# A decayed running sum behind a matrix product: the last four column blocks turned on TensorE, and the entry cut into finer pieces

## The chip, the cores and the metric

The kernel runs on one core of one Trainium2 chip. A core has five engines that work side by side, each through its own list in order: TensorE (PE, matmuls; its weight loads are shown as PEld), VectorE (DVE), ScalarE (ACT), GpSimd (POOL) and SyncE (SP, which here only issues transfers). 16 DMA engines move data between the main memory and the on-chip memory SBUF; TensorE writes into PSUM, a second on-chip memory of eight banks of 512 fp32 columns per partition. The metric is the device time of one execution in microseconds (us).

## The reference

```python
B, S, D = (16, 2048, 1024)
xw = x @ w                                   # x: (B, S, D), w: (D, D), float32
out[:, 0, :] = xw[:, 0, :]
for t in range(1, S):
    out[:, t, :] = decay * out[:, t - 1, :] + xw[:, t, :]    # decay: one factor per column
```

A matrix product, then along the time axis of each batch entry a recurrence with one decay factor per output column.

## The kernel before

**Tiling.** The 16 x 2048 rows are 64 chunks of 512 time steps. A chunk's product has 1024 columns, cut into eight slots n = 0 to 7 of 128 columns. A slot's column blocks are taken so that four times 32 columns of the output, 128 apart, make its 128 partitions. Slots 0 to 3 fill the lower half of the columns and slots 4 to 7 the upper half. The work of one slot is a step. In all groups but the last, a step covers two chunks (T = 1024 columns of PSUM, two banks); the last two chunks are worked one by one (T = 512), so that there are 31 x 8 + 16 = 264 steps. Negative numbers count steps from the end: -8 to -1 are the last chunk's slots.

**Into TensorE.** `load` fetches x on GpSimd's queue, cast to bf16. `turn` transposes it on VectorE in 32x32 blocks, reading pairs of bf16 as one fp32, and `part` copies it into `xt`, even and odd rows apart (ScalarE in the long run, both engines in the entry). `load_w` fetches the weights in pieces into the space of the output tiles, and `settle` copies them into `wsb`, as bf16, one copy for each row group k and half of the columns. A step is eight matmuls (k = 0 to 7) for each chunk.

**The recurrence.** PSUM holds the product with columns on partitions and time along the free axis. Slots of one kind (here called plain) are scanned by VectorE straight out of PSUM, 1024 steps in one `tensor_tensor_scan` (line 194). The others are paired: ScalarE copies the product to `xs` and multiplies the even steps by the decay, GpSimd adds these to the odd ones (line 174), VectorE scans the odd steps alone with the squared decay (line 180, half as long), and ScalarE and GpSimd fill in the even ones (lines 158 and 208). A plain slot's PSUM banks come free with VectorE's scan, a paired slot's with ScalarE's reads. `flips` names the steps that are the other kind than usual. The squared decays are in `dec2`, a PSUM tile that takes a bank.

**Out.** `back` transposes the result in 32x32 blocks on VectorE into an output tile, of which there are four in turn; when a half's four slots are there, `store` issues four transfers on SyncE, one for each group of 32 partitions, in runs of 128 columns (512 bytes). The last chunk's upper half is stored by two slots at a time, in runs of 64 columns (256 bytes).

**PSUM.** Of the eight banks, `ps` has three buffers of two banks in turn, `spare` one bank and `dec2` one.

**Order.** Every instruction is issued through `pin`, which keeps the order in which the program names it. That order is a list written by hand, `agenda`, of deeds for each step: letter and number, where P, S, C and B are a step's pairing, scan, completion and transposition back, T, X and Y the turning and copying of a chunk, W and w the weights' copies on VectorE and ScalarE, E, F and G the entry's turns and copies by halves of a chunk, M and U the first loads, D the decays and L one more load of x. Entry -99 is what comes before the first step, and steps without an entry follow `usual`. An engine takes its share of the list in this order and waits where an operand or a buffer isn't there. In the entry, TensorE first runs 34 matmuls on zeros (line 262), then chunk 0 for slots 0 to 3 (slot 3 in `spare`), by halves for the even k, then chunk 1 for slots 0 to 2, and slot 3's second half in the first of the `ps` buffers to come free.

Of the kernel before, what the change touches and what calls it, by code (L numbers as in the profile page):

```python
# [9 lines left out]
FP32 = mybir.dt.float32  # L10
# [15 lines left out]
def kernel(  # L26
# [60 lines left out]
        assert chunks[g[0]][0] == chunks[g[1]][0]  # L87

    dec = const.tile([128, K], FP32, name="dec")
    dec2 = psp.tile([128, 512], FP32, name="dec2")  # L90
    wsb = const.tile([128, K, K, NQ, P], BF16, name="wsb")
    wcols = wsb.rearrange("p k (h r) q i -> p k h q r i", h=2)

# [13 lines left out]
            in_=_ap(x, [[D, P], [P * D, j1 - j0], [1, CQ]],  # L107
                    (b * S + t0 + j0 * P) * D + q * CQ)))

    def turn(c, j0=0, j1=NJ):  # L110
        if c not in xw_of:
            xw_of[c] = ring(sb, "xw", 2, [128, M, NJ, P, 2], BF16)
        src = xb_of[c][:, j0:j1].rearrange("p j c -> p (j c)").bitcast(FP32)
        dst = xw_of[c].rearrange("p m j i e -> p (m j i e)").bitcast(FP32)
        pin(nc.vector.transpose(  # L115
            out=dst.rearrange("p (m j i) -> p j m i", m=M, i=P)[:, j0:j1],
            in_=src.rearrange("p (j m c) -> p j m c", m=M, c=P)))

    def part(c, copy, m0, m1, j0=0, j1=NJ):
        if c not in xt_of:  # L120
# [15 lines left out]
    class Tile:  # L136

        def __init__(self, g, n, ps, ot, there):  # L140
            self.b, self.t0 = chunks[g[0]]
            self.T = TL * len(g)
            self.n, self.ps, self.ot, self.there = n, ps, ot, there
            self.final = g == [nch - 1]
            self.paired = n % R != R - 1
            if len(tiles) in flips or len(tiles) - len(slots) in flips:
                self.paired = not self.paired
            self.so = ring(sb, "so", 4, [128, 2 * TL + 2])
            self.prev = None if self.t0 == 0 else last[n]
            if self.t0 + self.T < S:  # L150
                last[n] = const.tile([128, 1], FP32, name=f"keep{n}", bufs=2)
                self.keep = last[n]
            else:
                self.keep = None
# [22 lines left out]
        def scan(self):  # L177
            T, n, so = self.T, self.n, self.so
            if self.paired:
                pin(nc.vector.tensor_tensor_scan(  # L180
                    out=so[:, 3:T + 2:2],
                    data0=dec2[:, n:n + 1].to_broadcast([128, T // 2]),
                    data1=self.xs[:, 1:T:2],
                    initial=0.0 if self.prev is None else self.prev,
                    op0=ALU.mult,
                    op1=ALU.add,
                ))
            else:
                parts = self.ps if isinstance(self.ps, tuple) else (self.ps,)
                size = T // len(parts)  # L190
                before = 0.0 if self.prev is None else self.prev
                for i, ps in enumerate(parts):
                    t = 2 + i * size
                    pin(nc.vector.tensor_tensor_scan(  # L194
                        out=so[:, t:t + size],
                        data0=dec[:, n:n + 1].to_broadcast([128, size]),
                        data1=ps,
                        initial=before,
                        op0=ALU.mult,
                        op1=ALU.add,  # L200
                    ))
                    before = so[:, t + size - 1:t + size]
# [7 lines left out]
            if self.keep is not None:  # L210
                pin(nc.scalar.copy(out=self.keep, in_=so[:, T + 1:T + 2]))  # L211

        def back(self):
            T, n = self.T, self.n
            pin(nc.vector.transpose(  # L215
                out=self.ot[:, :, n % R * P:(n % R + 1) * P],
                in_=self.so[:, 2:T + 2].rearrange("p (i t) -> p i t", t=P)))
            self.there.add(n)
            size = 2 if self.final and n >= R else R
            n0 = n // size * size  # L220
            if self.there.issuperset(range(n0, n0 + size)):
                self.store(n0, n0 + size)

        def store(self, n0, n1):
            c0 = n0 % R * P
            size = (n1 - n0) * P
            for q in (0, 2, 1, 3):
                pin(nc.sync.dma_start(
                    out=_ap(out, [[D, P], [P * D, self.T // P], [1, size]],
                            (self.b * S + self.t0) * D + n0 // R * CH + q * CR + c0),  # L230
                    in_=self.ot[quad(q), :, c0:c0 + size]))


# [24 lines left out]
    rows = const.tile([128, 2, P], FP32, name="rows")  # L258
    pin(nc.vector.memset(idle, 0.0))  # L259
    pin(nc.vector.memset(rows, 0.0))  # L260
    for _ in range(34):
        pin(nc.tensor.matmul(out=spare, lhsT=idle[:, 0:128], rhs=idle, start=True, stop=True))  # L262
    H = NJ // 2
    halves = ((0, H), (H, NJ))
# [11 lines left out]
    def load_part(i):  # L276
        load_w(nc.gpsimd, *((0, 0, M // 2, M), (0, 1), (1, 0), (1, 1))[i])

    def settle_one(i, copy):
        settle(i // 8, i // 4 % 2, i % 4, copy)  # L280

    def decays(i):
        pin(nc.vector.transpose(out=cols, in_=rows))
        pin(nc.vector.tensor_copy(
            out=dec.rearrange("p (h r) -> p h r", h=2), in_=cols[:, :, 0:R]))
        pin(nc.vector.tensor_tensor(out=dec2[:, 0:K], in0=dec, in1=dec, op=ALU.mult))


    slots = [(g, n) for g in groups[:-1] for n in range(K)]
# [3 lines left out]
    def turn_and_load(c):  # L293
# [16 lines left out]
        "w": lambda i: settle_one(i, nc.scalar.copy),  # L310
        "M": load_half,
        "U": load_part,
        "E": lambda i: turn(i // 2, *halves[i % 2]),
        "F": lambda i: part(i // 2, nc.vector.tensor_copy, 0, 2, *halves[i % 2]),
        "G": lambda i: part(i // 2, nc.scalar.copy, 2, M, *halves[i % 2]),
        "f": lambda i: part(i // 2, nc.vector.tensor_copy, 2, M, *halves[i % 2]),
        "D": decays,
        "L": lambda i: load(*loads.pop(0)) if loads else None,
    }
    agenda = {  # L320
        -99: "M0 M1 U0 U1 M2 M3 U2 U3 L L L W0 w1 E0 F0 G0 w3 W2 E1 F1 G1 W4 w5 W6 w7 E2 F2 D G2 E3 F3 G3 W8 W9 W10 W11",
        0: "w12 L L w13 P0 S0",
        1: "w14 L P1 L",
        2: "S1 W15 P2 B0 S2",
        3: "T2 L S3 C0 C1 C2",
        4: "L P4 X2 L Y2 L B2 T3 B1 L",
        5: "P5 C3 X3 L S4",
        6: "B3 L Y3 S5 L P6 C5 C4 T4",
        7: "S7 S6 X4 L C7 C6 B5 B4 B7",
        8: "",  # L330
        9: "P8 B6 S8 P9 L L T5 C8",
        10: "P10 L L S9 L C9 L B8",
        11: "X5 S10 L C10 S11 B9",
        12: "P12 L B11 B10 C11 Y4",
        13: "P13 S12 T6 Y5 C12 L",
        14: "S13 P14 C13 L B12 L L",
        15: "S15 X6 S14 C14 B13",
        16: "L P16 B14 B15 Y6 L L",
        -16: "P-16 B-17 S-16 C-16 C-17",
        -15: "P-15",  # L340
        -14: "S-15 B-18 B-16 P-14",
        -13: "P-13 S-14 S-13 B-15",
# [6 lines left out]
        -6: "P-6 B-10 S-7 C-7 B-8",  # L349
        -5: "P-5 S-6 S-5",  # L350
        -4: "C-6 B-7 B-5 P-4 B-6",
        -3: "P-3 S-4 S-3",
        -2: "P-2 S-2 C-4 C-3 B-4",
        -1: "B-3 P-1 S-1 B-2 C-5 B-1 C-1 C-2",
    }
    flips = (0, 1, -2, -15, -8)
    later = {10: ["Y4"]}
    for c in range(5, nch):
        first = c // 2 * K
# [20 lines left out]
            deeds[deed[0]](int(deed[1:] or 0))  # L380

    perform(agenda[-99].split())
    for step, (g, n) in enumerate(slots):
        T = TL * len(g)
        if n % R == 0:
            ot, there = ot_tile(NJ * len(g)), set()
        if step == 0:
            heads = [ring(psp, "ps", 3, [128, T]) for _ in range(3)]
            firsts = [ps[:, 0:TL] for ps in heads] + [spare]
            for j0, j1 in halves:  # L390
                for k in range(0, K, 2):
                    for i in range(R):
                        matmul(firsts[i], i, k, xt_of[0], j0 * P, j1 * P)
            for k in range(1, K, 2):
                for i in range(R):
                    matmul(firsts[i], i, k, xt_of[0])
            for j0, j1 in halves:
                for i in range(3):
                    for k in range(K):
                        matmul(heads[i][:, TL:T], i, k, xt_of[1], j0 * P, j1 * P, j0 * P)  # L400
        if step < R:
            if n < 3:
                ps, second = heads[n], heads[n][:, TL:T]
            else:
                second = ring(psp, "ps", 3, [128, TL])
                ps = (spare, second)
            if n >= 3:
                for k in range(K):
                    matmul(second, n, k, xt_of[1])
        else:  # L410
            if len(g) == 2 or n % R < 3:
                ps = ring(psp, "ps", 3, [128, T])
            else:
                ps = ring(psp, "spare", 1, [128, TL])
            for k in range(K):
                for l, c in enumerate(g):
                    matmul(ps[:, l * TL:(l + 1) * TL], n, k, xt_of[c])
        tiles.append(Tile(g, n, ps, ot, there))
        left = step - len(slots)
        do = agenda.get(step, agenda.get(left) if left >= -2 * K else None)  # L420
        perform(usual(step) if do is None else do.split())
    assert not loads
# [28 lines left out]
```

## Time and profile before

| | us |
|---|---|
| time, median of 3 runs (lowest to highest) | 915.06 (914.53 to 915.75) |
| the profiled execution's own time | 914.25 |
| its span, from the first to the last instruction | 912.5 |
| TensorE, VectorE busy | 891.3, 826.0 |
| ScalarE, GpSimd busy | 685.8, 664.4 |
| start of the dummy matmuls; of the first real one | 1.20; 11.20 |
| end of the last matmul; of the last work on VectorE | 901.6; 905.6 |
| moved by DMA, mean rate | 204.49 MB, 224 GB/s |

A row of the timeline names the start, the time that the instructions of the row take together, engine, line, operation, what it writes and reads, the shape and the count; in brackets stands how long the engine was idle before and what ended that. The end of a matmul is modelled: one of 512 columns starts every 0.216 us while its row says about 0.38. A row of the table by stretches names the stretch, its length, busy us and count of instructions for PE, PEld, DVE, ACT and POOL, the clock granted to TensorE as a share of full speed, the mean busy share of the DMA engines (above 1 where packets of two queues are counted at once) and what they moved in GB/s. The slices cut the span into 40 equal parts; a digit is a share in tenths.

### The profile page before, as it was taken

What the parts mean: (1) busy time and instruction counts of PE and PEld (TensorE: products, weight loads), DVE (VectorE), ACT (ScalarE), POOL (GpSimd) and SP (SyncE); (2) the same over time, 40 slices, a digit from 0 to 9 for tenths busy, and PEclk for the clock granted to TensorE, in tenths of its full rate; (3) what the DMA queues carried; (4) which work ended last, traced back from release to release, by engine and by line L of the source; (5) the groups of instructions that cost most, each with busy time, mean ns of one, the idle gap of its engine ahead of it and who ended that gap; (6) DMA issues with size and microseconds to landing.
All of it is one profiled execution on the core that took longest, in us unless ns stands there. A gap on an engine that the chain in (4) does not pass through costs nothing.

```text
span 912.5 us, 11926 instructions
## 1 busy us (share of the span) xinstructions
PE 891.3 (98%) x4088; PEld 408.5 (45%) x4170; DVE 826.0 (91%) x613; ACT 685.8 (75%) x950; POOL 664.4 (73%) x764
## 2 busy tenths in 40 slices
PE   8899999999999999999999999999999999999995
PEld 4444444444444444444444444444444444444442
DVE  4999999999999999999999999999999999999986
ACT  3778887877877777778778778778778778777753
POOL 8688878777777777777677777777787776776552
PEclk9999999999999999999999999999999999999998
DMA  9999999999999999999999999999999999999668
GB/s 170 166 220 215 215 230 235 256 250 255 247 237 255 247 237 224 230 233 231 223 235 227 224 231 229 230 226 231 227 224 230 231 230 224 232 229 207 151 151 219
DMA packets 406253, 204.49 MB, mean 224 GB/s; under 512 B 12976, under 2 KB 405936, under 8 KB 406192
## 3 DMA queue, kind: packets, MB, share of 16 engines
q1 hardware_dynamic: 268848, 134.76, 59.5%
q0 software_dynamic: 137344, 68.96, 56.8%
q8 instruction: 32, 0.52, 0.2%
q14 instruction: 29, 0.24, 0.1%
HBM read 138.42 MB, written 134.22 MB: 299 GB/s over the span
## 4 chain that ended last, share of the span: by engine, by line
PE 90%; DMA 3%; POOL 2%; issue 2%; DVE 2%; ACT 1%; SPq 0%; DVEq 0%; POOLq 0%
PE ps L126 90%; DMA xb<-in_x_dram 2%; POOL xb L105 1%; DMA ot<-in_w_dram 1%; DVE so L194 1%; DVE xw L115 1%; POOL ot L245 1%; PE spare L126 0%; DMA out_dram<-ot 0%; DVE so L180 0%; POOL so L208 0%; ACT xt L123 0%; DVE ot L215 0%; POOL xs L174 0%; ACT xs L168 0%
## 5 line engine op out<-in xcount | busy, mean ns | idle before, releaser
L126 PE MATMUL ps<-xt,wsb 128*128 128x512 bf16 (+1 forms) x4011 | 874.2, 377 | 9.0 <-DVE so L194 2.6
L126 PEld LDWEIGHTS <-wsb 128*128 128x128 bf16 x4136 | 404.6, 98 | 485.7 <-issue 5.6
L174 POOL TENSOR_TENSOR xs<-h,xs 128x512 f32<-128x512 f32 (+1 forms) x193 | 245.3, 1271 | 195.5 <-ACT h L158 88.3
L168 ACT COPY xs<-ps 128x1024 f32<-128x1024 f32 (+1 forms) x193 | 191.6, 993 | 158.8 <-PE ps L126 149.3
L215 DVE STREAM_TRANSPOSE ot<-so 128x1024 f32<-128x1024 f32 (+1 forms) x264 | 302.7, 1184 | 1.9 <-POOL so L208 1.1
L208 POOL TENSOR_TENSOR so<-h,xs 128x512 f32<-128x512 f32 (+1 forms) x193 | 244.3, 1266 | 34.5 <-ACT h L158 18.1
L123 ACT COPY xt<-xw 128x2048 bf16<-128x2048 bf16 (+1 forms) x128 | 239.8, 1875 | 7.5 <-DVE xw L115 7.5
L105 POOL DMA_DIRECT2D xb<-in_x_dram x264 | 174.1, 660 | 2.0 <-POOLq L435 0.9
L158 ACT ACTIVATE h<-so,dec 128x512 f32<-128x512 f32 (+1 forms) x193 | 147.1, 763 | 36.0 <-DVE so L180 32.1
L115 DVE STREAM_TRANSPOSE xw<-xb 128x2048 f32<-128x2048 f32 (+1 forms) x66 | 146.7, 2222 | 6.1 <-DMA xb<-in_x_dram 6.1
L180 DVE TENSOR_TENSOR_SCAN so<-dec,keep,xs 128x512 f32<-128x512 f32 (+1 forms) x99 | 121.6, 1229 | 29.8 <-POOL xs L174 29.6
L180 DVE TENSOR_TENSOR_SCAN so<-dec,xs 128x512 f32<-128x512 f32 x94 | 114.8, 1222 | 31.3 <-POOL xs L174 28.2
L158 ACT ACTIVATE h<-ps,dec 128x512 f32<-128x512 f32 (+1 forms) x193 | 131.8, 683 | 0.0
L194 DVE TENSOR_TENSOR_SCAN so<-dec,ps 128x1024 f32<-128x1024 f32 x33 | 74.5, 2261 | 0.0
L194 DVE TENSOR_TENSOR_SCAN so<-dec,keep,ps 128x1024 f32<-128x1024 f32 (+1 forms) x33 | 73.4, 2225 | 0.0
L211 ACT COPY keep<-so 128x1 f32<-128x1 f32 x136 | 25.1, 187 | 0.3 <-DVE so L194 0.3
L173 ACT COPY so<-keep 128x1 f32<-128x1 f32 x99 | 19.0, 192 | 0.7 <-DVE ot L215 0.7
L171 POOL MEMSET so<- 128x1 f32 x94 | 11.0, 117 | 3.2 <-DVE ot L215 3.2
L262 PE MATMUL spare<-idle 128*128 128x512 bf16 x34 | 10.2, 473 | 1.2 <-DVE idle L259 1.2
L126 PE MATMUL spare<-xt,wsb 128*128 128x512 bf16 (+1 forms) x43 | 11.2, 359 | 0.1
L245 POOL DMA_DIRECT2D ot<-in_w_dram x16 | 9.0, 561 | 2.4 <-issue 0.7
L253 ACT COPY wsb<-ot 128x512 bf16<-128x512 bf16 x6 | 3.4, 615 | 5.7 <-DMA ot<-in_w_dram 5.7
(18 smaller groups left out, 20.3 us busy)
## 6 DMA issues: line engine op xcount, KB each, us to landing
out_dram<-ot SPq DMA_DIRECT2D x248, 512.0 KB, 10.6
xb<-in_x_dram POOLq DMA_DIRECT2D x248, 256.0 KB, 7.8
out_dram<-ot SPq DMA_DIRECT2D x12, 256.0 KB, 4.2
xb<-in_x_dram POOLq DMA_DIRECT2D x16, 128.0 KB, 5.0
ot<-in_w_dram POOLq DMA_DIRECT2D x12, 128.0 KB, 5.2
out_dram<-ot SPq DMA_DIRECT2D x8, 128.0 KB, 2.8
ot<-in_w_dram SPq DMA_DIRECT2D x4, 128.0 KB, 3.5
ot<-in_w_dram POOLq DMA_DIRECT2D x4, 64.0 KB, 4.3
```

The costliest lines, as they stand in the source:

```text
L105: pin(nc.gpsimd.dma_start(out=xb_of[c][quad(q), j0:j1], in_=_ap(x, [[D, P], [P * D, j1 - j0], [1, CQ]], (b * S + t0 + j0 * P) * D + q * CQ)))
L115: pin(nc.vector.transpose(out=dst.rearrange("p (m j i) -> p j m i", m=M, i=P)[:, j0:j1], in_=src.rearrange("p (j m c) -> p j m c", m=M, c=P)))
L123: pin(copy(out=xt_of[c][:, m0:m1, :, j0 * P:j1 * P], in_=src))
L126: pin(nc.tensor.matmul(out=ps[:, t0:t1], lhsT=wsb[:, k, n].rearrange("p q i -> p (q i)"), rhs=xt[:, k // 2, k % 2, t0:t1], start=(k == 0 a ...
L158: pin(nc.scalar.activation(out=h, in_=src, func=mybir.ActivationFunctionType.Copy, scale=dec[:, self.n:self.n + 1]))
L168: pin(nc.scalar.copy(out=self.xs, in_=self.ps))
L174: pin(nc.gpsimd.tensor_tensor(out=self.xs[:, 1:T:2], in0=g, in1=self.xs[:, 1:T:2], op=ALU.add))
L180: pin(nc.vector.tensor_tensor_scan(out=so[:, 3:T + 2:2], data0=dec2[:, n:n + 1].to_broadcast([128, T // 2]), data1=self.xs[:, 1:T:2], init ...
L194: pin(nc.vector.tensor_tensor_scan(out=so[:, t:t + size], data0=dec[:, n:n + 1].to_broadcast([128, size]), data1=ps, initial=before, op0=A ...
L208: pin(nc.gpsimd.tensor_tensor(out=so[:, 2:T + 2:2], in0=h, in1=self.xs[:, 0:T:2], op=ALU.add))
L211: pin(nc.scalar.copy(out=self.keep, in_=so[:, T + 1:T + 2]))
L215: pin(nc.vector.transpose(out=self.ot[:, :, n % R * P:(n % R + 1) * P], in_=self.so[:, 2:T + 2].rearrange("p (i t) -> p i t", t=P)))
```

## The change

Three parts. **The end:** the last chunk's slots 4 to 7 get no output tile. `cross` transposes their results on TensorE, in blocks of 128 columns x 128 steps against an identity that GpSimd makes at step -16, for two blocks of time at once and all four slots into one PSUM bank each; ScalarE and VectorE copy one bank each to SBUF with the columns in order, and two transfers of 256 KB in runs of 512 columns (2 KB) follow; then the same for the other two blocks. Step -3 becomes plain. **The entry:** 27 dummies instead of 34, a small ScalarE copy ahead of everything, turns of half the row pairs and copies of one row pair each, another order of the first matmuls and of the odd and even k up to step 8, and new lists for the steps up to 16. **The bank of the squares:** they lie in SBUF until step 8 and from then on in the bank `spare1`, which holds slot 3's second half in the entry and one of the transposes at the end. `store` and its bookkeeping move from `Tile` into a class `Outlet`, which changes nothing else in the stores that stay.

```diff
-    dec2 = psp.tile([128, 512], FP32, name="dec2")
+    squares = [const.tile([128, K], FP32, name="squares")]
...
-    for _ in range(34):
+    pin(nc.scalar.copy(out=idle[:, 0:1], in_=idle[:, 1:2]))
+    for _ in range(27):
...
+    def part_one(i, copy):
+        part(i // 8, copy, i % 4, i % 4 + 1, *halves[i // 4 % 2])
...
+    def square_again(i):
+        squares.append(ring(psp, "spare1", 1, [128, TL]))
+        square(0)
...
+    def cross(half):
+        b, t0 = chunks[-1]
+        nb = TL // 128 // 2
+        pts = [ring(psp, *(("spare1", 1) if half and i else ("ps", 3)), [128, R, 128])
+               for i in range(nb)]
+        wides = [ring(sb, *(("ot", 4), ("xb", 3))[half], [128, NQ, R, P]) for _ in range(nb)]
+        for r in (1, 0, 2, 3):
+            so = tiles[r - R].so
+            for i in range(nb):
+                t = 2 + (half * nb + i) * 128
+                pin(nc.tensor.transpose(out=pts[i][:, r], in_=so[:, t:t + 128], identity=ident))
+        for i, copy in enumerate((nc.scalar.copy, nc.vector.tensor_copy)):
+            pin(copy(out=wides[i].rearrange("p q r i -> p r q i"),
+                     in_=pts[i].rearrange("p r (q i) -> p r q i", q=NQ)))
+        for i in range(nb):
+            pin(nc.sync.dma_start(
+                out=_ap(out, [[D, 128], [1, CH]],
+                        (b * S + t0 + (half * nb + i) * 128) * D + CH),
+                in_=wides[i].rearrange("p q r i -> p (q r i)")))
...
-        -99: "M0 M1 U0 U1 M2 M3 U2 U3 L L L W0 w1 E0 F0 G0 w3 W2 E1 F1 G1 W4 w5 W6 w7 E2 F2 D G2 E3 F3 G3 W8 W9 W10 W11",
-        0: "w12 L L w13 P0 S0",
-        1: "w14 L P1 L",
-        2: "S1 W15 P2 B0 S2",
-        3: "T2 L S3 C0 C1 C2",
-        4: "L P4 X2 L Y2 L B2 T3 B1 L",
+        -99: "M0 M1 U0 U1 M2 M3 U2 U3 W0 w1 L E0 F0 G1 E1 L F2 D G3 E2 F4 L G5 W2 E3 F6 w3 G7 W4 W6 w5 w7 E4 F8 G9 E5 F10 G11 E6 F12 G13 E7 F14 G15 W8 W10 W9 W11",
+        0: "P0 L w15 w13",
+        1: "L L L S0 C0",
+        2: "L P2 P1 w12 S1 L L B0 B1 S2",
+        3: "w14 C2 T2",
+        4: "S3 P4 X2 Y2 T3 C1",
...
+        8: "C7 C6 L d P8 B4 B7 B6",
...
+        -16: "I P-16 B-17 S-16 C-16 C-17",
...
-        -3: "P-3 S-4 S-3",
-        -2: "P-2 S-2 C-4 C-3 B-4",
-        -1: "B-3 P-1 S-1 B-2 C-5 B-1 C-1 C-2",
+        -3: "S-3 S-4 C-4",
+        -2: "S-2",
+        -1: "S-1 V0 V1",
...
-    flips = (0, 1, -2, -15, -8)
+    flips = (0, 1, -2, -3, -15, -8)
...
+    spares = [spare] + [ring(psp, "spare1", 1, [128, TL])]
...
+            seconds = [ps[:, TL:T] for ps in heads] + [spares[1]]
             for j0, j1 in halves:
-                for k in range(0, K, 2):
+                for k in (0, 2):
                     for i in range(R):
                         matmul(firsts[i], i, k, xt_of[0], j0 * P, j1 * P)
-            for k in range(1, K, 2):
+            for k in (4, 6, 1, 3, 5, 7):
                 for i in range(R):
                     matmul(firsts[i], i, k, xt_of[0])
-            for j0, j1 in halves:
-                for i in range(3):
-                    for k in range(K):
-                        matmul(heads[i][:, TL:T], i, k, xt_of[1], j0 * P, j1 * P, j0 * P)
+            for k0 in range(0, K, 4):
+                for i in range(R):
+                    for k in range(k0, k0 + 4):
+                        matmul(seconds[i], i, k, xt_of[1], 0, H * P)
+            for i in range(R):
+                for k in range(K):
+                    matmul(seconds[i], i, k, xt_of[1], H * P, TL, H * P)
...
+            if step < K:
+                todo.sort(key=lambda kl: kl[0] % 2)
+            elif step == K:
+                todo.sort(key=lambda kl: kl[1])
```

In the new lists, E, F and G are numbered by quarters and eighths of a chunk (E: half of the row pairs; F and G: one row pair), d is `square_again`, I the identity and V `cross`.

## The prediction

> **What bounds the kernel now.** I read the busy shares first, then the slices, then TensorE in order of time at both ends, then the transfers at the end.
>
> ```profile
> span 912.5 us, 11926 instructions
> PE 891.3 (98%) x4088; PEld 408.5 (45%) x4170; DVE 826.0 (91%) x613; ACT 685.8 (75%) x950; POOL 664.4 (73%) x764
> PEclk9999999999999999999999999999999999999998
> DMA  9999999999999999999999999999999999999668
> ```
>
> The middle belongs to TensorE: 4096 matmuls of 512 columns, 8 in 1.73 us (0.216 each), are 884.3 us, and the records show hardly a gap between 37.7 and 901.6. Nothing in the change touches that stretch except where one scalar lies. So the span is 11.2 (until the first real matmul) + 884.3 + gaps + 10.9 (from the last matmul to the end); the gaps are left with about 6, all in the entry. The change works on the first and the last part alone.
>
> ```profile
> 1.20 10.17 PE L262 MATMUL spare<-idle 128*128 128x512 bf16 x34 [1.20 <-DVE idle L259]
> ...
> 8.60 1.25 DVE L115 STREAM_TRANSPOSE xw<-xb 128x1024 f32<-128x1024 f32 x1 [1.55 <-DMA xb<-in_x_dram]
> 9.88 0.69 DVE L123 COPY xt<-xw 128x1024 bf16<-128x1024 bf16 x1
> 9.88 1.05 ACT L123 COPY xt<-xw 128x1024 bf16<-128x1024 bf16 x1 [1.38 <-DVE xw L115]
> ...
> 15.70 0.53 DVE L253 COPY wsb<-ot 128x512 bf16<-128x512 bf16 x2 [0.87 <-DMA ot<-in_w_dram]
> ...
> 18.61 1.25 DVE L115 STREAM_TRANSPOSE xw<-xb 128x1024 f32<-128x1024 f32 x1 [2.38 <-DMA xb<-in_x_dram]
> ...
> 27.59 1.89 PE L126 MATMUL ps<-xt,wsb 128*128 128x512 bf16 x7 [1.25 <-DVE so L194]
> ...
> 29.77 7.07 PE L126 MATMUL ps<-xt,wsb 128*128 128x512 bf16 x32 [0.29 <-DVE so L194]
> ...
> 37.69 12.68 PE L126 MATMUL ps<-xt,wsb 128*128 128x512 bf16 x57 [0.86 <-DVE so L194]
> ```
>
> The operand is ready at 10.57, but the dummies hold TensorE until 11.20. Then it waits on landings (0.93 before 13.01, 1.00 before 14.89, 0.55 before 20.64, 0.31 before 23.56), and three times on a PSUM buffer that a scan still reads: 1.41 before 27.59, 0.45 before 29.77, 1.02 before 37.69.
>
> ```profile
> 899.69 1.89 PE L126 MATMUL spare<-xt,wsb 128*128 128x512 bf16 x8
> ...
> 903.12 1.24 DVE L194 TENSOR_TENSOR_SCAN so<-dec,keep,spare 128x512 f32<-128x512 f32 x1
> 904.28 1.27 DVE L215 STREAM_TRANSPOSE ot<-so 128x512 f32<-128x512 f32 x2
> ```
> ```profile
> 896.00:905.20 9.20, 5.58 (x26) 2.35 (x24) 8.32 (x12) 3.36 (x9) 3.69 (x5) 0.95 0.99 248
> 906.20:911.20 5.00, 0.00 (x0) 0.00 (x0) 0.00 (x0) 0.00 (x0) 0.00 (x0) 0.50 0.89 192
> ```
>
> The last two columns are DMA share and GB/s. No engine works after 905.6, yet the end is at 912.5: stores queue back to back from 883, in 512-byte runs at 248 GB/s, then 1.05 MB (slots 4 to 7) in 256-byte runs at 192, until 911.0. The end is bound by the DMA engines, not by VectorE.
>
> **The change, part by part.**
>
> *Fewer dummies, smaller pieces.* Seven dummies at 0.216 fewer: TensorE is free at 9.69. Half a turn takes 0.67 (the last transposes of this shape, 1.27 for two), half a copy 0.38 on VectorE, 0.62 on ScalarE (the 512-element copies there). Turn at 8.60, copy done 9.65, first matmul 9.70. Eight of 0.109 end at 10.57, then TensorE stands: the second half lands at 11.2 as before, turn and copy end at 12.3. Eight more to 13.2; the piece of the third row pair passes behind weight copy W2 (lands 12.6) and is ready at 13.9; eight whole matmuls to 15.65. The odd weight rows land at 15.66, copied at 16.0; sixteen matmuls end at 19.5, against 20.08 before. So most of the earlier start is only waited away.
>
> *Chunk 1 for four slots at once.* Slot 3's second half now has a bank of its own (the one that held the squares), so it no longer waits for a scan. Data lands at 18.6: TensorE starts at 19.7, does 64 half-width matmuls (7.0) and has all four slots by 26.7; before, the fourth came at 29.3. Step 4 still needs slot 0's scan: weight copies from 24.15 to 25.1, scan 2.26, so 27.4. Its even rows take 1.73, to 29.1; row 1 then needs w12, which the new list sets on ScalarE behind w15, w13 (from 27.16), a keep copy and slot 2's copies (1.00 + 0.69): done at 30.5. A wait of 1.4; the step ends at 32.3, against 33.2. Ahead 0.95.
>
> *After that.* The wait before step 6 (1.02) goes, as its bank is freed by ScalarE at 30.0: ahead 1.95. Step 9 needs step 6's bank, freed by ScalarE behind the copies of chunk 3 (turn ends about 40.1, then 3.8, then 0.97 and 1.7: 46.7), where TensorE arrives at 46.1: 0.7 lost. The 0.2 lost before 65.7 goes. Ahead 1.4. Chunks 5 and 6 are turned 0.1 us after landing; if they land no earlier, VectorE waits there, but their matmuls come 14 us and more later. SP and GpSimd issue the same loads.
>
> *The squares in SBUF.* Scans of slots 2, 4, 5 and 6 now read two SBUF operands beside GpSimd's adds, until step 8 puts the squares back into PSUM. The row: 1.22 us each, never longer where the squares lie in PSUM. The Trainium skill, "SBUF — State Buffer", section "Who interferes with whom", speaks against the change: a VectorE instruction with two SBUF inputs and a GpSimd one that reads SBUF exclude each other, the later one waiting for the whole of the earlier. By the row it costs nothing. By the rule, slot 4's scan (from about 41.2) meets an add until 42.0 and slot 6's one until 49.3, 1.2 us together; VectorE is 27.0 of 28.0 us busy there, yet TensorE pays only about 0.1, as ScalarE frees most banks. All four meeting a whole add (1.29 each) would cost 3.4. I take 0.1: head 1.3.
>
> *The end.* Removed: four transposes on VectorE (1.27 for two), slot 5's pair (ScalarE 0.59 + 0.48 + 0.53, GpSimd two of 0.74), eight stores. Added: slot 5's plain scan (1.25), 16 transposes on TensorE, four 128x512 copies out of PSUM (0.59 on ScalarE by its row there, VectorE alike), four stores of 256 KB. The identity (GpSimd, two instructions at step -16) lies in idle time of 2.2 us; behind it wait one add and one scan, which free no bank. Shifted by 1.3, the last matmul ends at 900.3, the last scan at 901.55 (the other three at 897.1, 899.0 and 900.2 start as their banks fill). Two transposes, copies 0.65: the first half's stores are issued at about 902.9, as SP gets through the earlier ones (902.38 + 1.28 - 1.3 = 902.4). Eight more transposes and copies: second half at 905.1. The DMA engines are busy with earlier data until 906.2 - 1.3 = 904.9 and with the first half until 906.7, so neither is late.
>
> No row shows a TensorE transpose of fp32. From below: one pass of 128 columns (0.109 for 256) plus an uncovered weight load (98 ns), 0.15. From above: four such passes at the half clock that the tail shows (0.50): 4 x (0.107 + 0.098) = 0.82. The Trainium skill, "TensorE: Matmul & The Clock Gate", Part 4, gives about 275 ns in a kernel's context (for bf16). I take 0.28; nothing hangs on it until 0.30.
>
> What is left is the rate of 1.05 MB. In the two stretches a 512-byte packet took 9.20 x 16 x 0.983 / 4578 = 31.6 ns, a 256-byte one 5.00 x 16 x 0.890 / 3870 = 18.4: 5.2 plus 51.6 per KB. 2 KB would be 110 ns: 512 packets on 16 engines, 3.6 us, instead of 5.0 (from 906.0 to 911.0). Less if 2-KB stores only reach 248 GB/s: 4.2, gain 0.8; more at the 2-KB reads of the entry: up to 2. I take 1.4.
>
> **Sum.** 1.3 + 1.4 = 2.7: span 909.8. The profiled execution took 914.25 and becomes 911.55; the median of the runs is 0.81 above it: 912.4.
>
> **Rivals.** *The head gives nothing* (w12 later than reckoned, the squares' scans blocked, or the clock falling back in the 1.8 us gap at 10.6): for it, VectorE's 27.0 of 28.0 us and the load-bound entry; against it, the 7 dummies and the freed bank stand in the trace. Time 915.06 - 1.4 = 913.7; with all four scans blocked, 915.6.
>
> *The stores are no faster*: the last 1.05 MB is limited by write receipts rather than packets. For it: the 512-byte stretch is not twice the 256-byte one. Then 915.06 - 1.3 = 913.7.
>
> *Slower: TensorE's transposes become the bound of the end.* Place: the eight of the second half stand behind the last two, all after the last scan. Price p each: the last stores are issued at 901.6 + 10p + 0.7, land about 3.3 later (1.2 to the first packet, 2 x 0.9, 0.3) and end 1.16 after that (911.3 to 912.46): 906.8 + 10p. It passes the forecast from p = 0.30, the old end from 0.57, 0.2% slower from 0.75. At 0.82 the span is 915.0, the time 917.6. For it: fp32 and a clock at half; against it: the clock fell only 2.7 us after the last matmul, so most turns still run at full clock.
>
> **How the numbers follow.** About 0.2% (1.8 us) can be told from no change. As worked out: 0.58 (own range 911.4 to 913.2). Head lost: 0.18. Stores no faster: 0.12. Transposes the bound: 0.08, half of it slower by over 0.2%. Both ends better (no wait for w12, stores at 390 GB/s; 910.3): 0.04. Faster 0.62, same 0.31, slower 0.07. Range 910.8 to 915.4.
>
> **What would show it.** First matmul at 9.7 and a gap to 12.3; no gap at 27.6 to 29.8 longer than 0.7, then one of 1.4 before row 1 of step 4; step 8 starting near 42.7; the last matmul ending near 900.3; no store packets missing between 883 and the end, and 2-KB packets of about 110 ns. Wrong if the transposes last over 0.3 us, if the DMA engines stand idle after 902, if scans on squares in SBUF exceed 1.3 us, or if the clock row dips in the first slice.

## The result, and the profile after

| | before | after |
|---|---|---|
| time, median (lowest to highest) of 6 runs each | 915.22 (914.53 to 915.75) | 911.03 (910.09 to 911.6) |
| the profiled execution: its time; its span | 914.25; 912.5 | 911.6; 909.8 |
| first real matmul; end of the last one | 11.20; 901.58 | 9.83; 901.21 |
| from the last matmul to the end of the span | 10.9 | 8.6 |

The ratio after to before is 0.9953, with a 95% interval of 0.994 to 0.9966: faster by 4.2 us. The forecast was 2.7 faster, 912.4 with a range of 910.8 to 915.4, and the time lies within that range, but below the forecast's own range for its likeliest case (911.4 to 913.2). The two profiled executions lie at opposite ends of their scatter (914.25 is under all six timed runs of before, 911.6 is the slowest of the six of after), so the pair of spans, 912.5 and 909.8, understates the difference. That the second equals the forecast's span of 909.8 is luck.

The page after, the same four lines as before: span, busy shares, granted clock and DMA share by slices.

```profile
span 909.8 us, 11956 instructions
...
PE 890.9 (98%) x4097; PEld 409.1 (45%) x4179; DVE 827.0 (91%) x619; ACT 686.5 (75%) x954; POOL 662.9 (73%) x764
...
PEclk9999999999999999999999999999999999999999
DMA  9999999999999999999999999999999999999758
```

The middle is as it was, 98% of TensorE. In the last slices the clock row no longer ends in an 8, because the clock now falls late against the shorter end (at 906.3, where the span ends at 909.8; before at 904.3 of 912.5).

The entry after, rows of the timeline (start, time taken, engine, line, operation, shape, count, and in brackets the idle time before with its releaser):

```profile
0.74 1.28 ACT L272 ACT_TABLE_LOAD   x1 [0.74 <-PEq L494]
...
2.28 7.39 PE L274 MATMUL spare<-idle 128*128 128x512 bf16 x27 [2.28 <-ACT idle L272]
...
9.83 0.49 PE L126 MATMUL ps<-xt,wsb 128*128 128x256 bf16 x3 [0.15 <-DVE xt L123]
...
12.93 0.49 PE L126 MATMUL ps<-xt,wsb 128*128 128x256 bf16 x3 [2.06 <-DVE xt L123]
...
16.48 0.49 DVE L264 COPY wsb<-ot 128x512 bf16<-128x512 bf16 x2 [2.33 <-DMA ot<-in_w_dram]
...
16.83 0.82 PE L126 MATMUL ps<-xt,wsb 128*128 128x512 bf16 x3 [0.74 <-DVE wsb L264]
...
28.08 1.89 PE L126 MATMUL ps<-xt,wsb 128*128 128x512 bf16 x7 [0.22 <-DVE so L193]
...
31.02 15.71 PE L126 MATMUL ps<-xt,wsb 128*128 128x512 bf16 x71 [1.05 <-ACT wsb L264]
...
47.13 3.18 PE L126 MATMUL ps<-xt,wsb 128*128 128x512 bf16 x14 [0.40 <-ACT h L157]
```

Against the rows before (27.59, 29.77 and 37.69, each after a wait for a scan), one short wait for a scan is left in the entry, at 28.08; new are the gap until 12.93, the one for w12 at 31.02 and the small one at 47.13. All four were forecast, at 12.3, 27.4, 30.5 and 46.1 to 46.8. The totals for the whole kernel stand in the view of TensorE's waits (what waited, for what: us in total, times, longest), first before, then after:

```profile
PE ps L126 <- DVE so L194: 2.6, 4, 1.2
PE ps L126 <- DVE xt L123: 1.2, 2, 0.8
PE spare L262 <- DVE idle L259: 1.2, 1, 1.2
PE ps L126 <- DVE wsb L253: 0.8, 1, 0.8
```
```profile
PE ps L126 <- DVE xt L123: 2.7, 4, 2.1
PE spare L274 <- ACT idle L272: 2.3, 1, 2.3
PE ps L126 <- ACT wsb L264: 1.1, 1, 1.1
PE ps L126 <- DVE so L193: 1.0, 2, 0.8
PE ps L126 <- DVE wsb L264: 0.7, 1, 0.7
```

Waits for scans fall from 2.6 to 1.0, and waits for the turned x and for weights rise from 2.0 to 4.5: the earlier start of the matmuls is given back to the loads, as forecast. (One of the two waits for scans that are left lies behind the entry, at 92.97; it comes up again below.)

The end after, timeline again:

```profile
899.32 1.89 PE L126 MATMUL spare<-xt,wsb 128*128 128x512 bf16 x8
901.05 1.11 PE L330 MATMUL ps<-ident,so 128*128 128x128 f32 x6
902.59 0.55 PE L330 MATMUL ps<-ident,so 128*128 128x128 f32 x3 [0.43 <-DVE so L193]
...
902.95 0.58 ACT L332 COPY ot<-ps 128x512 f32<-128x512 f32 x1 [2.33 <-DMA out_dram<-ot]
...
903.06 0.69 DVE L332 COPY ot<-ps 128x512 f32<-128x512 f32 x1 [0.53 <-PE ps L330]
...
903.56 1.44 SPq L335 DMA_DIRECT2D out_dram<-ot  x2
...
905.10 0.98 SPq L335 DMA_DIRECT2D out_dram<-xb  x2
```

And the table by stretches (stretch, length, busy us and count for PE, PEld, DVE, ACT and POOL, granted clock, DMA share, GB/s):

```profile
896.00:904.60 8.60, 7.40 (x41) 3.93 (x38) 7.81 (x10) 2.73 (x6) 2.15 (x3) 1.00 0.98 251
904.70:908.60 3.90, 0.00 (x0) 0.00 (x0) 0.00 (x0) 0.00 (x0) 0.00 (x0) 0.70 0.79 280
```

The transposes and copies are done by 904.6, and no gap of the DMA engines opens ahead of the last stores (0.98 busy until 904.6). In the last stretch the mean rate is 280 GB/s where it was 192. It isn't even: in the one microsecond from 906.21 the engines are full (a share of 1.03) and move 385 GB/s, in the next one they run empty (0.60 and 227).

### The profile page after: what moved, and what is told of

Same layout as the page of the kernel before. It is cut to its first block, busy times and chain, and to the rows that moved or that the text cites. A ratio compares the mean times of both kernels' runs of the same rounds, so it can differ in the third digit from the quotient of the medians.

```text
span 909.8 us, 11956 instructions
## 1 busy us (share of the span) xinstructions
PE 890.9 (98%) x4097; PEld 409.1 (45%) x4179; DVE 827.0 (91%) x619; ACT 686.5 (75%) x954; POOL 662.9 (73%) x764
## 4 chain that ended last, share of the span: by engine, by line
PE 89%; DMA 4%; DVE 3%; issue 2%; POOL 1%; SPq 0%; DVEq 0%; POOLq 0%
PE ps L126 88%; DMA xb<-in_x_dram 2%; DMA out_dram<-ot 1%; DVE ot L218 1%; DVE so L193 1%; POOL ot L256 1%; PE spare L126 1%; DVE so L179 1%; DMA ot<-in_w_dram 1%; DVE xw L115 1%; SPq L239 0%; POOL xb L105 0%; PE ps L330 0%; DVE xb L332 0%; PE spare L330 0%
## 5 line engine op out<-in xcount | busy, mean ns | idle before, releaser
L179 DVE TENSOR_TENSOR_SCAN so<-spare,keep,xs 128x512 f32<-128x512 f32 (+1 forms) x98 | 120.8, 1233 | 28.4 <-POOL xs L173 28.1
L179 DVE TENSOR_TENSOR_SCAN so<-spare,xs 128x512 f32<-128x512 f32 x90 | 110.0, 1222 | 30.7 <-POOL xs L173 27.8
L172 ACT COPY so<-keep 128x1 f32<-128x1 f32 x98 | 18.7, 191 | 1.5 <-DVE ot L218 1.5
L126 PE MATMUL spare<-xt,wsb 128*128 128x512 bf16 (+1 forms) x58 | 13.2, 342 | 0.1
L170 POOL MEMSET so<- 128x1 f32 x94 | 10.9, 116 | 1.1 <-ACT keep L210 1.1
L274 PE MATMUL spare<-idle 128*128 128x512 bf16 x27 | 7.4, 441 | 2.3 <-ACT idle L272 2.3
```

What stands on the lines that cost most here:

```text
L126: pin(nc.tensor.matmul(out=ps[:, t0:t1], lhsT=wsb[:, k, n].rearrange("p q i -> p (q i)"), rhs=xt[:, k // 2, k % 2, t0:t1], start=(k == 0 a ...
L179: pin(nc.vector.tensor_tensor_scan(out=so[:, 3:T + 2:2], data0=squares[-1][:, n:n + 1].to_broadcast([128, T // 2]), data1=self.xs[:, 1:T:2 ...
```

## The experiments

Every ratio here is to runs of the kernel before that were timed beside it: 915.0 (21 runs, 914.34 to 916.53) for the first four experiments, 914.89 (10 runs, 914.22 to 916.7) for the last four, on another chip.

**Both kernels once more**, unedited, to see how much of one trace repeats.

> The kernel before once more, for a second profile. Theory: the first profiled execution (914.25) was a fast one against a median of 915.2, so this one's last matmul ends later than 901.6, at about 902.5, and the time from there to the end stays 10.9. Rival: the end varies and the entry doesn't: last matmul at 901.6 and more than 10.9 after it.

> The changed kernel once more, to see which of its gaps come again. Theory: the profiled execution was a slow one (911.6, the slowest of six), because the odd weight rows landed 1 us late (14.2 after 12.6, 0.6 before the change). Expected 911.0, ratio 0.9954, and a profile whose last matmul ends near 900 rather than 901.3. Rival: the late landing belongs to the new order of the entry; then it is there again and the last matmul ends at 901.3.

Before: one execution, 915.69. After: 911.06 (4 runs, 910.62 to 911.39), ratio 0.9957 (0.9943 to 0.997). For before the expectation held: the last matmul ends at 902.83, and 11.1 us follow. For after it held in the time and not in its reason: the odd weight rows came later still, and the last matmul nevertheless ended earlier, at 900.56. What the first execution had lost is a wait at 92.97, taken up below. The waits of the entry come back, at other sizes. TensorE before, then after:

```profile
28.42 1.89 PE L126 MATMUL ps<-xt,wsb 128*128 128x512 bf16 x7 [1.25 <-DVE so L194]
...
38.85 11.38 PE L126 MATMUL ps<-xt,wsb 128*128 128x512 bf16 x51 [1.19 <-DVE so L194]
```
```profile
28.40 1.89 PE L126 MATMUL ps<-xt,wsb 128*128 128x512 bf16 x7 [0.35 <-DVE so L193]
...
31.39 15.71 PE L126 MATMUL ps<-xt,wsb 128*128 128x512 bf16 x71 [1.10 <-ACT wsb L264]
```

In this execution of before, TensorE is 0.8 later than in the first one at 28.42 and 1.2 later at 38.85 (27.59 and 37.69 there). What moved is the loads: VectorE's copy of the early odd weight rows, which waits for their landing, started at 16.93 instead of 15.70. The start of that copy is a yardstick of how late the loads came in an execution. Taken off the end of the last matmul (the column "difference"), it makes executions comparable that were lucky and unlucky with their loads:

| execution | entry | copy of the odd rows, us | last matmul ends, us | difference | from there to the end of the span |
|---|---|---|---|---|---|
| before | old | 15.70 | 901.58 | 885.9 | 10.9 |
| before, once more | old | 16.93 | 902.83 | 885.9 | 11.1 |
| new end alone | old | 15.47 | 901.79 | 886.3 | 9.0 |
| new entry alone | new | 17.03 | 900.85 | 883.8 | 10.7 |
| after | new | 16.48 | 901.21 | 884.7 | 8.6 |
| after, once more | new | 16.94 | 900.56 | 883.6 | 8.5 |
| 256-byte runs | new | 16.38 | 900.56 | 884.2 | 9.8 |
| 34 dummies | new | 15.79 | 899.46 | 883.7 | 8.4 |
| w12 first | new | 16.41 | 900.65 | 884.2 | 8.8 |

By this the new entry is worth 886.0 - 884.0 = 2.0, the means of three and six. Should the new entry itself make these loads later (the copy starts at 16.0 on average in the three executions and at 16.5 in the six), about 0.5 of that would be its own cost; so few executions can't tell, but the timed runs below speak for the whole. The first pair of profiles showed only 901.58 - 901.21 = 0.37 of it, because its execution of before had its loads 0.8 earlier than its execution of after.

**Each half alone.** The new entry with the old end. The lists of the end are put back, as here, and with them the output tile of the last four slots, stored by two slots at a time, and no identity is made:

```diff
-        -3: "S-3 S-4 C-4",
-        -2: "S-2",
-        -1: "S-1 V0 V1",
+        -3: "P-3 S-4 S-3",
+        -2: "P-2 S-2 C-4 C-3 B-4",
+        -1: "B-3 P-1 S-1 B-2 C-5 B-1 C-1 C-2",
...
-    flips = (0, 1, -2, -3, -15, -8)
+    flips = (0, 1, -2, -15, -8)
...
```

> The new entry with the old end (paired slots, transposes on VectorE, stores in 256-byte runs). Theory: the end alone gives 2.1 to 2.4, so the entry gives the rest of 4.2, about 1.9: 913.3. Rival, by the two profiles as they stand (last matmul only 0.4 earlier): 914.8. Second rival, the forecast's split (1.3): 913.9.

The old entry with the new end: `cross`, the identity, no output tile for the last four slots, and as `spare1` the bank that the squares keep until then:

```diff
-        -16: "P-16 B-17 S-16 C-16 C-17",
+        -16: "I P-16 B-17 S-16 C-16 C-17",
...
-        -3: "P-3 S-4 S-3",
-        -2: "P-2 S-2 C-4 C-3 B-4",
-        -1: "B-3 P-1 S-1 B-2 C-5 B-1 C-1 C-2",
+        -3: "S-3 S-4 C-4",
+        -2: "S-2",
+        -1: "S-1 V0 V1",
...
-    flips = (0, 1, -2, -15, -8)
+    flips = (0, 1, -2, -3, -15, -8)
```

> The old entry with the new end. Theory: the 2-KB stores take 3.0 us for what took 5.0 and nothing else is late: 2.1 to 2.4 less, 913.0. By the forecast's term (1.4): 913.8. Rival, that nearly all of the gain is the end: 911.4.

New entry alone: 912.69 (11 runs, 911.76 to 913.74), ratio 0.9975 (0.9966 to 0.9983), 2.3 faster, more than the theory (1.9) and the forecast (1.3) had it. New end alone: 913.49 (11 runs, 911.96 to 914.41), ratio 0.9982 (0.9973 to 0.9991), 1.5 faster, between the forecast's 1.4 and the theory's 2.1 to 2.4. They add up to 3.8, and both together gave 3.9 in the same series; within these intervals no interplay of the halves shows. The step from the new entry alone to both gives the end once more: 912.69 - 911.06 = 1.6. The traces put the end at about 2.3 (10.7 to 11.1 against 8.4 to 9.0, last column), more than the timed 1.5 and 1.6, but inside the first one's interval of 0.8 to 2.5.

**Long runs or the other route?** The end does two things: it goes through TensorE instead of VectorE, and it stores 2 KB at a time. Keeping the first and giving up the second, each 256-KB transfer becomes two of 128 KB in runs of 256 bytes:

```diff
-            pin(nc.sync.dma_start(
-                out=_ap(out, [[D, 128], [1, CH]],
-                        (b * S + t0 + (half * nb + i) * 128) * D + CH),
-                in_=wides[i].rearrange("p q r i -> p (q r i)")))
+            for odd in range(2):
+                pin(nc.sync.dma_start(
+                    out=_ap(out, [[D, 128], [128, 4], [1, 64]],
+                            (b * S + t0 + (half * nb + i) * 128) * D + CH + odd * 64),
+                    in_=wides[i].rearrange("p q r i -> p (q r i)").rearrange(
+                        "p (a o c) -> p a o c", o=2, c=64)[:, :, odd]))
```

> The changed kernel with the turned blocks stored in runs of 256 bytes, by eight transfers of 128 KB as before the change; turning, copies and order stay. Theory (the end is bound by packets): 4096 packets of 18.6 ns on 16 DMA engines take 4.8 us where 512 of 86 ns take 2.8, so 2.0 more: 913.0, and the last matmul where it was. Rival (the gain comes from the shorter chain after the last scan): 911.0.

912.15 (6 runs, 911.61 to 913.16), ratio 0.9971 (0.996 to 0.9983): 1.1 of the 3.9 is lost, about halfway between the theory and its rival, so neither holds alone. The stretches of its end, and below them that of the old end behind the new entry:

```profile
896.00:903.80 7.80, 6.74 (x38) 3.64 (x35) 7.02 (x9) 2.17 (x5) 1.50 (x3) 1.00 1.00 259
903.90:908.90 5.00, 0.00 (x0) 0.00 (x0) 0.07 (x1) 0.00 (x0) 0.00 (x0) 0.74 1.02 211
```
```profile
904.20:910.20 6.00, 0.00 (x0) 0.00 (x0) 0.63 (x2) 0.00 (x0) 0.00 (x0) 0.50 0.89 195
```

From the last matmul to the end it takes 9.8, between the old end's 10.9 and the new one's 8.5. Read from these traces, the length of the runs carries 1.3 of 2.4 and the route 1.1. The timed medians divide their 1.6 otherwise: 912.69 with the old end, 912.15 with the new route in short runs, 911.06 with long ones, so 1.1 for the length and 0.5 for the route.

The packets show why the trace flatters the route. At the last matmul, 0.80 MB of the earlier 512-byte stores were still to move in this execution, against 0.94 to 1.01 in those of the old end and 0.91 to 0.95 in the two of after, whose order up to there is the same. A tenth of a megabyte is 0.4 us at the 248 GB/s of such stores. The rest of the route's part goes with fuller DMA engines, a share of 1.02 at 256 bytes against 0.89, as the data is ready earlier: a reading of these rows, not a thing that an experiment separated (the old route also reads each transfer from 32 partitions, the new one from 128). So the longer runs are the larger part, 1.1 to about 1.8, and the route is worth between 0.5 and 1.1. A little of the length's part lies behind the last packet: the span ends 1.5 us after it in the four executions with 256-byte stores, and 1.25 us after it in the six with 2-KB ones.

**The dummies.** The clock was one of the forecast's worries, with only 27 dummies and then a gap. With the 34 of before:

```diff
-    for _ in range(27):
+    for _ in range(34):
```

> The changed kernel with 34 dummy matmuls again. Theory (the earlier start is waited away, since TensorE stands 1.9 to 2.2 us until the second half of chunk 0 is copied): first matmul 1.5 later, second group where it was, 911.0. Rival (the seven dummies are part of the gain): 912.5.

910.36 (4 runs, 909.6 to 910.6), ratio 0.995 (0.9935 to 0.9965). TensorE starts 2 us later and loses nothing:

```profile
2.29 9.78 PE L274 MATMUL spare<-idle 128*128 128x512 bf16 x34 [2.29 <-ACT idle L272]
11.91 0.49 PE L126 MATMUL ps<-xt,wsb 128*128 128x256 bf16 x3
...
14.03 0.81 PE L126 MATMUL ps<-xt,wsb 128*128 128x512 bf16 x2 [0.22 <-DVE xt L123]
```

The gap of 2.2 that after has ahead of 12.93 is filled by dummies here. So taking out the seven dummies is worth nothing, and the first matmul's time says nothing of the entry. This execution is the shortest of all (span 907.8), but in the table it stands where after's second one does (883.7 and 883.6): its loads came early. Whether 0.7 of the time is real is not settled, as the ranges of the timed runs touch.

**The wait for w12.** The changed kernel waits 1.2 before 31.02 for w12, the weights of row 1 for the upper half of the columns, which ScalarE copies late. Copied first:

```diff
-        0: "P0 L w15 w13",
+        0: "P0 L w15 w13 w12",
...
-        2: "L P2 P1 w12 S1 L L B0 B1 S2",
+        2: "L P2 P1 S1 L L B0 B1 S2",
```

> The changed kernel with the weight copy w12 set ahead of slot 2's copies on ScalarE. Theory: the wait of 1.2 us in step 4 shrinks to about 0.2 (w12 done at 29.5 instead of 30.9), slot 2's chain is 0.6 later without holding TensorE, and about 0.8 is left at the end: 910.2. Rival (the loads of the first 90 us set the pace, so TensorE only waits later): 911.0.

910.62 (5 runs, 910.39 to 913.26), ratio 0.9958 (0.9945 to 0.9971), within the scatter of after. The wait only moves; ScalarE, then TensorE:

```profile
27.80 1.66 ACT L264 COPY wsb<-ot 128x512 bf16<-128x512 bf16 x3 [3.50 <-DMA ot<-in_w_dram]
29.45 1.00 ACT L167 COPY xs<-ps 128x1024 f32<-128x1024 f32 x1
...
30.94 0.61 ACT L264 COPY wsb<-ot 128x512 bf16<-128x512 bf16 x1
...
31.60 2.76 PE L126 MATMUL ps<-xt,wsb 128*128 128x512 bf16 x12 [1.06 <-ACT wsb L264]
```

Now w12 is there at 29.5, and w14 is late: it stands behind slot 2's copies, and row 5 waits for it until 31.60. The theory that w12 alone sets this wait fell; it is whichever weight copy comes first behind slot 2's copies on ScalarE. Both ahead of slot 2's copies was not tried.

**The squares.** The forecast set two SBUF operands against GpSimd's adds at 0.1. To see the price without its small exposure, the squares stay in SBUF for the whole kernel:

```diff
-        8: "C7 C6 L d P8 B4 B7 B6",
+        8: "C7 C6 L P8 B4 B7 B6",
```

> The changed kernel with the squared decays left in SBUF to the end, so that all 190 paired scans read two SBUF operands. By the skill's rule (a scan waits for the whole of an add that began first): the mean paired scan well above 1.22 us, some over 2.4, VectorE, busy 91% already, late, and TensorE waiting for banks and chunks: 915 to 960. By the row (scans of 1.18 to 1.22 in the entry but one): 911.0.

One execution: 915.43, span 913.6. Scans of 512 odd steps at line 179 (min, median, max ns, then first and last start), in after with the squares in SBUF and then in PSUM, and below them in this kernel:

```profile
L179 DVE TENSOR_TENSOR_SCAN so<-squares,xs x4: 1176/1188/1918, 32.4 to 50.2; 128x512 f32<-128x512 f32 x4
...
L179 DVE TENSOR_TENSOR_SCAN so<-spare,xs x90: 1184/1225/1227, 82.7 to 873.2; 128x512 f32<-128x512 f32 x90
```
```profile
L179 DVE TENSOR_TENSOR_SCAN so<-squares,xs x94: 1175/1449/2770, 32.5 to 876.2; 128x512 f32<-128x512 f32 x94
```

With the squares in PSUM no scan of this form exceeds 1.227; without that the median is 1.449 and the longest 2.77. The rule that the prediction cited is borne out, here with a second operand that is one column repeated: 60 of the 94 scans began while GpSimd was adding, and each of them ended 1.08 us after that addition did, whether 0.2 or 1.2 us of it were left. Of the other 34, 33 took 1.18 to 1.20. In the kernel after it met one scan of four, slot 4's: 1.918 at 41.69, 0.73 over the row, beside an add from 41.23 to 42.53. No wait of TensorE followed from it. Kept for the whole kernel, it makes VectorE 890 us busy instead of 827, makes TensorE wait 3.6 for a scan before 96.02 and costs 4.4 us (915.43 against 911.06, on different chips; the last matmul ends 888.5 after the yardstick instead of 884.0).

## Why the prediction was right or wrong

**Right in the mechanism, too small in the sum.** The forecast had 1.3 for the head and 1.4 for the end. Timed alone, they were worth 2.3 and 1.5; in the traces, 2.0 and 2.3. The head was too small by both measures (the timed interval is 1.6 to 3.1). The end was right by the timed runs and too small by the traces. The sum of 2.7 was 4.2.

**The end: the packet was mis-sized.** "2 KB would be 110 ns" was a line through two points, 256 and 512 bytes, drawn out to four times the larger. In both executions of after the 512 packets of 2 KB took 86 ns each, packet by packet. 512 on 16 engines are 2.8 us, not 3.6, and 5.0 - 2.8 = 2.2 is near the 2.3 of the traces. The nearer row was the one that the forecast kept for the upper end of its gain, the 2-KB reads of the entry ("up to 2"). Yet the agreement hides two errors of opposite sign, which the run with 256-byte runs shows. A gain of 0.5 to 1.1 comes with the route, at a packet that is no shorter (19.6 ns each after 18.7). And of the 2.2 that the longer packets save with 16 engines full, the trace of that run shows 1.3 and the timed runs 1.1. The forecast took the DMA engines as the whole of the end and as full; they were 0.89 busy in its old last stretch and are 0.79 busy in the new one.

**The head: right step by step until 36, then several terms a little too dear, and one loss missed.** Measured from the yardstick, forecast and after agree: step 4 comes 11.7 and 11.6 after the copy of the odd rows, row 1 14.8 and 14.5. At step 6 after was 2.3 ahead of before (37.69 - 15.70 = 22.0 against 31.02 + 24 x 0.216 - 16.48 = 19.7), where the forecast had 2.0. The wait before step 9 cost 0.56 and 0.49 in the two executions for a forecast 0.7, and before's wait near 66, which goes, was 0.39 and 0.49 for a forecast 0.2. So the second pair of executions ends 885.9 - 883.6 = 2.3 apart, 1.0 above the forecast's 1.3, by differences of 0.1 to 0.3 each.

In the first execution of after another 0.95 is lost at 92.97, and 1.15 is left. The forecast excluded this loss: it said of chunks 5 and 6 that their matmuls come 14 us after the landing, and stopped there. Chunk 7 is the one that came late:

```profile
85.08 2.31 DVE L115 STREAM_TRANSPOSE xw<-xb 128x2048 f32<-128x2048 f32 x1 [1.17 <-DMA xb<-in_x_dram]
...
92.97 2.32 PE L126 MATMUL ps<-xt,wsb 128*128 128x512 bf16 x10 [0.78 <-DVE so L193]
```

Its last load was issued at 77.05 instead of 67.67, the data landed at 84.96 instead of 80.94, VectorE stood 1.17 with everything behind it late, and a scan freed its bank too late for TensorE. That chain is read from the trace; no run took it away. The other executions fit it: in the second one of after the same load was issued at 76.62 and landed at 83.77, and TensorE ran through. Of the six executions in the table with the new entry, three lose time at this place (0.95, 0.31 in the new entry alone, 0.29 with w12 first) and three none.

**First matmul 9.7, gap to 12.3, third row pair 13.9**: 9.83, 12.93, 14.20. Right in kind. The gap is 0.6 longer, and not for a late landing: the second half of chunk 0 landed at 11.21, as forecast. The forecast left out D, the decays' three small instructions, which stand ahead of the turn on VectorE (10.84 to 11.55), and the copy behind it took 0.57 instead of 0.38. **The new ScalarE copy** was costed at nothing and is not: the dummies wait for it, and start at 2.28 instead of 1.20, behind a load of ScalarE's tables that takes 1.28. They still end before x is there, since the clock was granted at 5.1 instead of 6.6 in that execution. In the second execution it was granted at 7.1, and the dummies held TensorE until 10.48, with the copies of x done at 10.30; the gap that follows swallowed it. What the forecast also didn't see is the copy's use: before the change the same load of tables stood at 6.59, ahead of ScalarE's first weight copy at 7.88, which now starts at 6.48.

**Squares 0.1**: slot 4's scan was caught as the rule said, slot 6's not, and TensorE paid nothing visible. Right, though that scan's 1.92 us is over the 1.3 that the forecast had named as a sign of being wrong: the sign was set too tight for what the forecast itself expected of this scan.

**Slow transposes, the rival on the other side.** The 16 transposes' time was bounded by 0.15 and 0.82 us and taken as 0.28. The line's own rows (durations min, median, max):

```profile
L330 PE MATMUL ps<-ident,so x12: 272/273/330, 901.0 to 903.5; 128*128 128x128 f32 x12
L330 PEld LDWEIGHTS ps<-ident,so x12: 139/141/143, 900.8 to 903.4; 128*128 128x128 f32 x12
```

One lasts 273 ns by its modelled end, but those behind the last scan start every 0.11 us (902.97, 903.08, 903.19 and so on), with weight loads of 0.14 that overlap them, and the clock was still full. So the price per transpose was 0.11, under the lower bound, and the rival never came near its point of 0.30. The 275 ns that the Trainium skill gives for bf16 ("TensorE: Matmul & The Clock Gate", Part 4) is about the length of one here, not the pace of many: the measurement decides.

**Stores no faster, and head worth nothing** are the other two rivals. The first falls by the 192 and 280 GB/s and by the run with 256-byte runs, the second by the new entry alone, 2.3 faster.

## What to carry to other kernels

Where the last transfers set the end, cost them by packets: the same megabyte took about 4.9 us of the 16 DMA engines in 256-byte packets and 2.8 in 2-KB ones, and a few transposes on a TensorE that has just become idle are a cheap way to get there. A single profile of an entry that is bound by loads can be lucky by a microsecond; before a forecast rests on its gaps, take off a yardstick such as the landing of the last early weight. And when loads are reordered, follow every one of them to the point where it is needed, not only the next few.

## What was not expected of the hardware

**Early loads scatter.** Over ten executions of the eight kernels, the early odd weights' copy began between 15.47 and 17.03, with the same loads ahead of it but for small shifts in issue. The end of the last matmul went with it, to within 0.4 us in the three executions with the old entry and 1.1 us in the six of the table with the new one.

**The clock can fall in the entry.** In the new end's kernel with the old entry, TensorE waited 1.46 and 0.99 us for loads, the second time before 14.76, and then ran at half clock for 3.4 us:

```profile
8.00:14.90 6.90, 4.63 (x30) 2.58 (x28) 4.08 (x5) 3.01 (x4) 6.33 (x12) 1.00 1.30 189
14.90:18.30 3.40, 3.31 (x16) 2.33 (x16) 0.64 (x2) 1.29 (x3) 3.18 (x6) 0.50 1.36 175
18.30:22.00 3.70, 3.62 (x19) 1.80 (x19) 2.85 (x6) 1.04 (x1) 2.53 (x6) 1.00 1.30 172
```

16 matmuls of 256 columns took 0.216 each instead of 0.109, 1.7 us in place; by the table of differences 0.4 of it reached the end, as the next stage waited for loads and scans anyway. The one gap of about 2 us in the new entry, longer than either, brought no such fall in any of its traces.

The times of the clock's changes suggest why. In all ten executions every change comes a whole multiple of 3.413 us after the first grant: the fall behind the last matmul after 263 to 265 of them, this one after 3 (10.24 us), and its end after 4. Cut into such stretches, the one ahead of this fall (11.50 to 14.91) holds nearly all of both waits, and TensorE stood idle for 70% of it. In the other entries the emptiest stretch was idle for 60% (new entry alone, 9.61 to 13.02), and the clock stayed; in the profiled execution of after a border at 11.97 cuts the gap in two, 46% and 40%. With the squares in SBUF even the gap of 3.8 us ahead of 96.02 brought no fall: a border at 93.99 cuts it into 51% and 60%. By these traces it is the idle share of such a stretch that counts, not the length of one gap, with the limit somewhere between 60% and 70%. That is read from a single fall, and no run was made to bring it about.
